# Attention reordered in a hybrid encoder: rotations ahead of scores, values in halves, a second sum buffer, tail masks on TensorE, rstd by product, and a changed cost rule in the static scheduler

## The chip, the cores and the metric

The kernel runs on the eight cores of one Trainium2 chip, one sequence per core, without exchange between the cores. The metric is the device time of the slowest core in microseconds (us). Executions in the usual, fast state agree within about 0.3%. Some executions fall in a slower state, in which the cores of one die get a lower clock; they are marked and left out of every comparison. A ratio is the mean time of one kernel's fast runs over that of the other's of the same rounds, so it isn't quite the ratio of the medians that are quoted.

## The reference, cut to what matters

```python
# x: (8, 2048, 1024); 15 heads of 64 in 3 groups, dilation 1, 4, 16, a band of +-64 keys each
def dilated_attention_mixer(h, w_qkv, q_norm, k_norm, w_o):
    q, k, v = split(h @ w_qkv)
    q = rope(rms_norm(q, q_norm), pos); k = rope(rms_norm(k, k_norm), pos)
    # per group: banded softmax attention over each residue class of positions
    ...
    wts = softmax(stack(lses), axis=0)      # groups weighted by their denominators
    return concat(outs * wts) @ w_o

for i in range(2):                          # layer 0: attention, layer 1: short convolution
    x = x + mixer_i(rms_norm(x))
    x = x + sq_relu_mlp(rms_norm(x))        # 1024 -> 4096 -> 1024
return rms_norm(x)
```

The weights of the groups are proportional to their denominators, so that a group need not be normalized by itself: its exp-weighted values are divided by the sum of all three denominators. The kernel keeps one running sum of denominators (`dtot`) and multiplies by its reciprocal at the end.

## The kernel before: the parts that matter

The program is a list of operations with data ranges, costs and priorities. A list scheduler in Python orders them for each engine before anything runs. The order of each engine's instructions is fixed from then on.

```python
    def schedule(self):
        ...
        while len(order) < n:
            # the engine that can start earliest; on it, the ready operation of lowest priority number
            ...
            o.eng, o.fn, o.cost = alt
            free[e] = t + o.cost
            ...
    def c_dve(n, fast):
        return 0.16 + (0.00053 if fast else 0.00104) * n
```

The heads are worked through in eight units. Units 0 to 5 hold two heads (two lanes) of one group; unit 6 holds two single heads, one with dilation 4 and one with 16; unit 7 holds the last head. A unit's queries and keys are projected, then rotated and normalized (rstd below is the reciprocal root of the mean square, by which they are multiplied):

```python
        def rope_a(u):
            ...                              # swap copy of neighbouring rows by DMA, squares
            MMS(mms, [CRS, sq.r(...)], [PR(b)])          # sums of squares, 8 products of 128x512
            ACT(ln, PS(b), AF.Ln, ...)
            ACT(rs.ap, ln, AF.Exp, ..., scale=-0.5, ps=False)
            DMA("sp", scr_d[u % 2]..., rs.ap[0:61:4, :], ...)          # to DRAM
            for h in range(2):
                DMA("sp", rbc.ap[64 * h:64 * h + 64, 0:n],
                    scr_d[u % 2, h:h + 1, 0:n].broadcast_to([64, n]), ...)   # and back, broadcast
```

The attention of a unit goes in steps of 1024 score columns: scores on PE, exp on ACT, the band mask as a multiplication on DVE, then the output and denominator products on PE into one pair of PSUM banks, which is evicted after each block of 512 positions:

```python
        pp = _Ring([0, 1]); pS = _Ring([2, 4]); pO = (6, 7)       # PSUM banks
        dtot = B(U_DT, 4096, True)
            ...
                ACT(P.ap, psum[:, 512 * sb:512 * sb + 1024], AF.Exp, ..., scale=0.125)
                for (lo, n_, map_, shp) in ml:
                    TT("dve", pv, pv, map_, ALU.mult, ...)         # band mask
        def finalize(units, lo, n):                                # 1/den and its products
            ACT(a, a, AF.Ln, ...); ACT(a, a, AF.Exp, ..., scale=-1.0, ps=False)
            for u in units:
                TT("dve", o, o, dtot.ap[rows, lo:lo + n], ALU.mult, ...)
```

The fillers and the priorities (a lower number goes first):

```python
        p.pri = 1000 * u + 300       # projections and rotation of unit u
        p.pri = 1000 * u             # scores, exp, masks, outputs of unit u
        fill = v_tiles(1, 300); mark = {0: 3}; fill += proj_tiles(1); ...
```

## Time and profile before

| | before |
|---|---|
| time | 1521.54 us median of 3 (1520.95 to 1522.93) |
| PE busy | 95% of the span |
| PE without work, 245 to 330 us | 20 us (median of the cores) |
| TensorE clock at half, 240 to 330 us | 54.6 us (median of the cores) |
| first Relu eviction of the first MLP | 383.2 us (median of the cores) |
| from there to the start of the last matmul | 1124.9 us |

The last two rows cut the run in two, at the first activation of the first MLP. They are read from each core's trace.

The page of the profile, the slowest core (core 6), in 40 equal slices; the digits are tenths busy, and PEclk is the granted TensorE clock in tenths:

```profile
PE 1450.2 (95%) x7207; PEld 675.1 (44%) x7207; DVE 636.2 (42%) x818; ACT 492.5 (32%) x779; POOL 526.7 (35%) x492
...
PE   4999997699999999999998999998999999999996
...
PEclk9999998589999999999999999999999999999998
```

There is one visible hole, around 250 us, with a clock dip. The table of stretches there (columns: stretch in us, its length, then busy time and instruction count of PE, weight load, DVE, ACT, POOL, then the granted clock, the DMA share, GB/s):

```profile
240.00:250.00 10.00, 10.00 (x79) 4.58 (x78) 5.93 (x8) 6.58 (x10) 0.00 (x0) 1.00 0.19 57
250.00:260.00 10.00, 3.70 (x40) 1.82 (x38) 8.16 (x11) 7.44 (x13) 1.61 (x2) 0.71 0.60 118
260.00:270.00 10.00, 4.21 (x12) 1.47 (x12) 6.04 (x11) 1.22 (x3) 0.00 (x0) 0.67 1.10 184
270.00:280.00 10.00, 7.07 (x26) 2.93 (x27) 7.48 (x8) 4.15 (x5) 1.54 (x2) 0.50 0.68 211
280.00:290.00 10.00, 8.37 (x31) 3.55 (x28) 4.96 (x6) 4.05 (x4) 0.75 (x1) 0.50 0.50 173
290.00:300.00 10.00, 6.22 (x23) 2.50 (x22) 5.69 (x6) 3.16 (x3) 2.66 (x5) 0.50 0.61 184
300.00:310.00 10.00, 7.71 (x34) 3.89 (x34) 2.97 (x6) 3.68 (x5) 0.93 (x2) 0.50 0.64 184
310.00:320.00 10.00, 10.00 (x41) 4.17 (x40) 3.47 (x7) 3.50 (x5) 0.75 (x1) 0.72 0.33 107
```

PE is idle in part and at half clock from 270 to 310 us. The chain of work that ended last tells why (start, us, what; in order of time):

```profile
253.48 16.50 DMA arena<-scr
...
271.21 1.23 DVE arena L333
...
272.58 1.10 PE psum L317 x4
...
286.40 1.30 ACT arena L343
...
287.94 2.77 PE psum L317 x8
```

The broadcast read of unit 6's rstd from DRAM takes 16.5 us, then the rotation ends, then PE gets its scores; from there evictions (L343) and 8 output products alternate.

The rest of the run has smaller gaps. The timeline of PE alone after 420 us (start, length, what, count; in brackets the idle time before and what ended it):

```profile
419.71 396.08 PE L317 MATMUL psum<-arena 128*128 128x512 bf16 x1834
818.76 14.19 PE L317 MATMUL psum<-arena 128*128 128x512 bf16 x65 [2.97 <-POOL arena L333]
836.43 208.03 PE L317 MATMUL psum<-arena 128*128 128x512 bf16 x962 [3.48 <-POOL arena L970]
1046.50 14.40 PE L317 MATMUL psum<-arena 128*128 128x512 bf16 x66 [2.04 <-POOL arena L333]
1062.96 429.97 PE L317 MATMUL psum<-arena 128*128 128x512 bf16 x2003 [2.06 <-POOL arena L333]
1496.71 13.22 PE L317 MATMUL psum<-arena 128*128 128x512 bf16 x104 [3.78 <-POOL arena L333]
```

Five gaps, 14.3 us together, each behind a norm. On the median core PE is idle for 11.7 us after 420 us, and its clock is at half for 13.7 us between the first Relu and the last matmul, in periods that begin in these gaps or within 1 us behind them. The timeline of all engines just before the first of them:

```profile
814.62 0.74 DVE L336 SCALAR_TENSOR_TENSOR arena<-arena 128x512 bf16<-128x512 f32 x1
...
815.28 0.68 DVE L333 TENSOR_TENSOR arena<-arena,psum 128x512 f32<-128x512 f32 x1
815.68 2.94 POOL L333 TENSOR_TENSOR arena<-arena 128x512 f32<-128x512 f32 x2 [2.13 <-ACT arena L433]
815.88 3.29 DVE L336 SCALAR_TENSOR_TENSOR arena<-arena 128x512 bf16<-128x512 f32 x2
```

An STT takes 0.74 us while POOL is idle and 1.65 us (3.29 for two) while POOL adds. The scheduler before reckons it as 0.16 + 0.00104 x 512 + 0.06 = 0.75 us in either case. The Trainium skill, "SBUF — State Buffer", section "Who interferes with whom", says that an instruction of the vector engine with two inputs in SBUF contends with a POOL instruction that reads SBUF, since the two share a port. This trace agrees: 0.74 against 1.65 us.

### The profile page before, as it was taken

What the parts mean: (1) busy time and instruction counts of PE and PEld (TensorE: products, weight loads), DVE (VectorE), ACT (ScalarE), POOL (GpSimd) and SP (SyncE); (2) the same over time, 40 slices, a digit from 0 to 9 for tenths busy, and PEclk for the clock granted to TensorE, in tenths of its full rate; (3) what the DMA queues carried; (4) which work ended last, traced back from release to release, by engine and by line L of the source; (5) the groups of instructions that cost most, each with busy time, mean ns of one, the idle gap of its engine ahead of it and who ended that gap; (6) DMA issues with size and microseconds to landing.
All of it is one profiled execution on the core that took longest, in us unless ns stands there. A gap on an engine that the chain in (4) does not pass through costs nothing.

```text
span 1520.2 us, 20021 instructions; the slowest of 8 cores (1513.7 to 1520.2 us)
## 1 busy us (share of the span) xinstructions
PE 1450.2 (95%) x7207; PEld 675.1 (44%) x7207; DVE 636.2 (42%) x818; ACT 492.5 (32%) x779; POOL 526.7 (35%) x492
## 2 busy tenths in 40 slices
PE   4999997699999999999998999998999999999996
PEld 1656443233444444444443444443444444444444
DVE  3647677459413023023049534459223022032058
ACT  3566676343310310310333333333310300301333
POOL 5100000136730630621666222256621621612652
PEclk9999998589999999999999999999999999999998
DMA  9944444630510510411310333311411312213014
GB/s 250 186 91 98 93 110 105 187 85 1 83 29 1 83 28 8 77 29 20 57 22 8 55 42 49 56 29 17 67 28 20 65 28 39 44 28 56 1 56 167
DMA packets 60912, 95.01 MB, mean 62 GB/s; under 512 B 3792, under 2 KB 40912, under 8 KB 58768
## 3 DMA queue, kind: packets, MB, share of 16 engines
q0 software_dynamic: 52016, 69.18, 26.0%
q1 hardware_dynamic: 8800, 24.55, 5.4%
q8 instruction: 60, 0.98, 0.3%
q14 instruction: 36, 0.29, 0.1%
HBM read 127.37 MB, written 8.52 MB: 89 GB/s over the span
## 4 chain that ended last, share of the span: by engine, by line
PE 88%; DVE 4%; DMA 3%; issue 2%; POOL 1%; ACT 1%; SPq 0%; POOLq 0%; DVEq 0%; ACTq 0%
PE psum L317 88%; DVE arena L336 2%; DMA arena<-scr 2%; DMA arena<-xT 2%; DVE arena L333 1%; POOL arena L333 1%; ACT arena L328 1%; POOL arena L349 0%; ACT arena L343 0%; ACT arena L433 0%; SPq L349 0%; DMA outT<-arena 0%; DMA scr<-arena 0%; POOLq L282 0%; POOL arena L449 0%
## 5 line engine op out<-in xcount | busy, mean ns | idle before, releaser
L317 PE MATMUL psum<-arena 128*128 128x512 bf16 (+6 forms) x7207 | 1450.2, 366 | 60.4 <-DVE arena L333 15.3
L317 PEld LDWEIGHTS psum<-arena 128*128 128x128 bf16 (+2 forms) x7207 | 675.1, 101 | 835.3 <-issue 145.5
L333 DVE TENSOR_TENSOR arena<-arena,psum 128x512 f32<-128x512 f32 (+1 forms) x384 | 259.4, 682 | 752.8 <-PE psum L317 749.0
L333 POOL TENSOR_TENSOR arena<-arena 128x512 bf16<-128x512 bf16 (+2 forms) x393 | 449.3, 1147 | 326.8 <-ACT arena L328 144.2
L328 ACT ACTIVATE arena<-psum 128x512 bf16<-128x512 f32 (+1 forms) x306 | 202.0, 668 | 636.6 <-PE psum L317 620.4
L336 DVE SCALAR_TENSOR_TENSOR arena<-arena 128x512 bf16<-128x512 f32 (+2 forms) x232 | 221.2, 995 | 23.1 <-ACT arena L328 18.4
L333 DVE TENSOR_TENSOR arena<-arena 128x2048 bf16<-128x2048 bf16 (+4 forms) x146 | 128.0, 921 | 35.9 <-ACT arena L328 25.1
L349 POOL DMA_DIRECT2D arena<-wdn x16 | 12.5, 781 | 318.6 <-PE psum L317 318.6
L343 ACT CAST arena<-psum 128x512 bf16<-128x512 f32 (+2 forms) x149 | 87.0, 590 | 96.1 <-PE psum L317 91.2
L433 ACT ACTIVATE arena<-arena 128x512 f32<-128x512 f32 x115 | 72.1, 629 | 141.7 <-DVE arena L333 138.3
L328 ACT ACTIVATE arena<-arena 128x512 f32<-128x512 f32 (+2 forms) x85 | 54.3, 656 | 67.8 <-DVE arena L333 55.6
L349 POOL DMA_DIRECT2D arena<-xT x18 | 13.4, 766 | 91.7 <-DVE arena L333 72.4
L349 POOL DMA_DIRECT2D arena<-wqk x8 | 7.4, 925 | 86.8 <-PE psum L317 86.8
L345 DVE CAST arena<-psum 128x512 bf16<-128x512 f32 (+2 forms) x27 | 18.4, 683 | 39.5 <-PE psum L317 39.3
L343 ACT COPY arena<-psum 128x512 f32<-128x512 f32 x38 | 22.8, 600 | 36.7 <-PE psum L317 36.7
L349 POOL DMA_DIRECT2D arena<-wup x16 | 15.0, 938 | 47.2 <-PE psum L317 42.4
L328 ACT ACTIVATE arena<-psum,arena 128x512 f32<-128x512 f32 (+1 forms) x29 | 19.4, 668 | 18.2 <-PE psum L317 18.0
L538 ACT ACTIVATE arena<-arena 128x1024 bf16<-128x1024 bf16 x23 | 24.1, 1057 | 1.9 <-DVE arena L345 0.7
L349 POOL DMA_DIRECT2D arena<-wo x8 | 4.3, 549 | 52.1 <-PE psum L317 52.1
L449 POOL TENSOR_TENSOR arena<-arena 128x512 bf16<-128x512 f32 x8 | 10.8, 1355 | 19.4 <-DMA arena<-xT 19.4
L448 ACT ACTIVATE arena<-arena 128x512 bf16<-128x512 f32 (+1 forms) x30 | 14.2, 525 | 9.9 <-DVE arena L333 6.6
L449 DVE TENSOR_TENSOR arena<-arena 128x512 bf16<-128x512 f32 (+1 forms) x10 | 6.6, 679 | 14.9 <-DMA arena<-xT 14.7
(16 smaller groups left out, 38.6 us busy)
## 6 DMA issues: line engine op xcount, KB each, us to landing
arena<-wup POOLq DMA_DIRECT2D x16, 1024.0 KB, 8.7
arena<-wdn POOLq DMA_DIRECT2D x16, 1024.0 KB, 11.8
arena<-xT POOLq DMA_DIRECT2D x14, 1024.0 KB, 9.2
arena<-arena SPq DMA_DIRECT2D x14, 512.0 KB, 6.3
arena<-scr SPq DMA_DIRECT2D x14, 512.0 KB, 6.6
arena<-win POOLq DMA_DIRECT2D x8, 768.0 KB, 7.4
outT<-arena SPq DMA_DIRECT2D x24, 256.0 KB, 3.0
arena<-wqk POOLq DMA_DIRECT2D x7, 512.0 KB, 11.2
```

What stands on the lines that cost most here:

```text
L317: i = e.matmul(o, lhsT=l, rhs=r, start=s0, stop=s1, skip_group_check=True)
L328: return p.op("act", lambda e: e.activation(out=out, in_=in_, func=func, **kw), R, W, c_act(n, ps) + (0.09 if scale is not None and not is ...
L333: return p.op(eng, lambda e: e.tensor_tensor(out=out, in0=in0, in1=in1, op=op), R, W, cost)
L336: return p.op("dve", lambda e: e.scalar_tensor_tensor(out=out, in0=in0, scalar=scalar, in1=in1, op0=op0, op1=op1), R, W, c_dve(n, False) + ...
L343: alts.append(("act", lambda e: e.copy(out=out, in_=in_), c_act(n) + more))
L345: alts.append((e_, lambda e: e.tensor_copy(out=out, in_=in_), c_dve(n, False) + more))
L349: return p.op(eng, lambda e: e.dma_start(out=out, in_=in_), R, W, 1.3 if eng == "sp" else 1.0, chan=chan, fill=fill, nbytes=nbytes)
L433: p.op([("act", lambda e, o=o, i=xa: e.activation(out=o, in_=i, func=AF.Square), c_act(n, False)), ("dve", lambda e, o=o, i=xa: e.tensor_t ...
L448: alts = [("act", lambda e, o=o, i=xa: e.activation(out=o, in_=i, func=AF.Square), c_act(n, False)), ("dve", lambda e, o=o, i=xa: e.tensor ...
L449: ("dve", lambda e, o=o, i=xa: e.tensor_tensor(out=o, in0=i, in1=i, op=ALU.mult), c_dve(n, False))]
L538: ("act", lambda e, o=sq.ap[:, sl], i_=rw.ap[:, sl]: e.activation(out=o, in_=i_, func=AF.Square), c_act(1024, False))], None, [rw.r(*rr)], ...
```

## The change

The attention's idle time is to be filled, and the scheduler is to know costs that it didn't know. In full the change

- orders units as (group, pair) = (0,0), (1,0), (2,0), (1,1), (0,1), (2,1), takes the values of groups 1 and 2 in halves between the projections, and gives projections, rotations and final products priorities of their own;
- computes the rstd of units 6 and 7 by a block-diagonal product that leaves the mean on all rows, so that Ln and Exp yield the broadcast form without DRAM;
- masks units 4 to 7 by a product of the identity with a bias of 0 or -30000, accumulated before the scores;
- gives unit 7 its own swap and rstd buffers and drops its key copy; gives units 6 and 7 a second sum buffer, on the normed input; moves buffers of x;
- in the scheduler, charges DVE and POOL more when both work from SBUF (contention rule), and doubles PE's cost while its recent load is low (clock rule).

The diff, cut to its core:

```diff
+UNITS = [(0, 0), (1, 0), (2, 0), (1, 1), (0, 1), (2, 1)]
+PMU = 4
+FILL = 'v11 v10 p1 v20 p2 v21 p3 p4 p5 p6 p7'.split()
+AHEAD = [6, 1, 6, 1, 0, 1, 3, 5]
+PRI_P = [-50, 950, 1950, 2950, 3950, 4950, 5950, 6950]
+PRI_R = [-150, -100, 900, 2300, 2900, 4950, 4900, 6650]
+PRI_V = [0, 800, -140]
+PRI_F = [6900, 7900]
+PEB = 6
 ... in schedule():
             o.eng, o.fn, o.cost = alt
+            if o.sbuf and e in both and o.chan is None:
+                over = min(o.cost, max(0.0, both["pool" if e == "dve" else "dve"] - t))
+                o.cost += (0.4 if e == "dve" else 0.15) * over
+                both[e] = t + o.cost
+            if e == "pe":
+                ...                          # load of the last 4 us
+                if full and load < 0.5 and t > 25:
+                    full = False
+                elif load > 0.93:
+                    full = True
+                if not full:
+                    o.cost *= 2
 ... in rope_a():
+            if u >= PEB:
+                for j in range(4 * nw):
+                    b = pp.next()
+                    MMS([(PS(b), bd64.ap, sq.ap[:, sl], True, True)], ...)
+                    ACT(PS(b), PS(b), AF.Ln, ..., 512, bias=eps_ap)
+                    ACT(rbc.ap[:, sl], PS(b), AF.Exp, ..., 512, scale=-0.5)
+                return
 ... in attention():
+                for q in range(2 if on_pe else 0):
+                    mms.append((PS(sb + q), ident.ap, map_, True, False))
-                                    kv(kb.ap[hs(h)]), qv(qb.ap[hs(h)]), True, True))
+                                    kv(kb.ap[hs(h)]), qv(qb.ap[hs(h)]), not on_pe, True))
 ... buffers:
-        dtot = B(U_DT, 4096, True)
+        dtots = [B(U_DT, 4096, True), B(U_HT + 12288, 4096, True)]
+        sws = [B(U_X + 8192, 4096)] * 7 + [B(U_W + 4096, 2048)]
+        rbcs = [B(U_X + 12288, 4096)] * 7 + [B(U_X + 22528, 2048)]
 ... (cuts: loads of the new constants, buffers of x, weight loads held until unit 7 is rotated)
```

More of the change, by code (lines that the diff above doesn't have):

```diff
@@ L25 @@
 CELL = 64
+UNITS = [(0, 0), (1, 0), (2, 0), (1, 1), (0, 1), (2, 1)]
[7 more added lines that the diff above has]
+PEB = 6
 PS_BASE = 1 << 20
 class _Op:
-    __slots__ = ("alts", "eng", "fn", "cost", "chan", "fill", "nbytes", "deps", "idx", "pri",
+    __slots__ = ("sbuf", "alts", "eng", "fn", "cost", "chan", "fill", "nbytes", "deps", "idx", "pri",
                  "pos", "sig", "sig_idx", "succ", "nwait", "ready", "start", "done", "waits")
@@ L61, in op @@
         pe = o.eng == "pe"
+        o.sbuf = all(r[1] < PS_BASE for r in reads)
         rc = list(self.cells(reads))
@@ L109, in schedule @@
         free = {e: 0.0 for e in self.ENGS}
+        both = {"dve": 0.0, "pool": 0.0}
+        hist, h0, full = [], 0, True
         qfree = {"sp": 0.0, "pool": 0.0}
@@ L132, in schedule @@
             o.eng, o.fn, o.cost = alt
+            if o.sbuf and e in both and o.chan is None:
[3 more added lines that the diff above has]
+            if e == "pe":
+                while h0 < len(hist) and hist[h0][1] < t - 4:
+                    h0 += 1
+                load = sum(min(b, t) - max(a, t - 4) for a, b in hist[h0:]) / 4
+                if full and load < 0.5 and t > 25:
[4 more added lines that the diff above has]
+                    o.cost *= 2
+                hist.append((t, t + o.cost))
             free[e] = t + o.cost
@@ L266, in build_nc @@
     cst_d = din("cst", [128, NCST])
+    bd_d = din("bd", [128, 128])
+    bias_d = din("bias", [128, NCST - C_MB + 128])
     rope_d = din("rope", [2, 128, T])
@@ L366, in build_nc @@
         tabs = [B(U_X + 2048 * i, 2048) for i in range(4)]
-        sw = B(U_X + 8192, 4096)
-        rbc = B(U_X + 12288, 4096)
+        sws = [B(U_X + 8192, 4096)] * 7 + [B(U_W + 4096, 2048)]
+        rbcs = [B(U_X + 12288, 4096)] * 7 + [B(U_X + 22528, 2048)]
         sq = B(U_OT + 12288, 4096)
@@ L371, in build_nc @@
         qk = [[B(U_X + 24576 + 2048 * (2 * i + w), 2048) for w in range(2)] for i in range(2)]
+        bd64, ident = B(U_RS + 1024, 128), B(U_RS + 1152, 128)
         rst = [B(U_RS + 512 * i, 512) for i in range(2)]
-        xparts = [[(U_X + 16384, 4), (U_X + 22528, 2), (U_X + 10240, 2)],
-                  [(U_X + 20480, 2), (U_X + 8192, 2), (U_X + 12288, 4)],
+        xparts = [[(U_X + 16384, 4), (U_X + 8192, 4)],
+                  [(U_X + 12288, 4), (U_X + 20480, 4)],
                   [(U_X, 8)], [(U_X + 24576, 8)]]
@@ L404, in xs, with load_w @@
             return b.ap[:, lo:lo + n], b.r(lo, lo + n)
-        def load_w(buf, dview, kc, cols_, chan):
+        def load_w(buf, dview, kc, cols_, chan, after=None):
             o = buf.ap[:, 0:kc * cols_].rearrange("p (c f) -> p c f", c=kc)
-            DMA("pool", o, dview.rearrange("(c p) f -> p c f", p=128), [], [buf.r(0, kc * cols_)],
-                chan, nfill(chan), 128 * kc * cols_ * 4)
+            d = DMA("pool", o, dview.rearrange("(c p) f -> p c f", p=128), [], [buf.r(0, kc * cols_)],
+                    chan, nfill(chan), 128 * kc * cols_ * 4)
+            if after is not None:
+                d.deps.add(after)
             return o
@@ L503, in build_nc @@
             128 * (NCST - C_SEL) * 4)
+        DMA("pool", bd64.ap, bd_d, [], [bd64.r()], "bd", 0, 1 << 16)
         load_wv(1)
@@ L524, in rope_a @@
         def rope_a(u):
-            rw = raws[u % 2]
+            rw, sw, rbc = raws[u % 2], sws[u], rbcs[u]
             nw = 2 if u < 7 else 1
             n = 2048 * nw
-            f = nfill("sw")
+            f = nfill("sw%d" % (u // 7))
             for q in range(2):
                 DMA("sp", sw.ap[q:127 + q:2, 0:n], rw.ap[1 - q:128 - q:2, 0:n], [rw.r(0, n)], [sw.r(0, n)],
-                    "sw", f, 128 * n)
+                    "sw%d" % (u // 7), f, 128 * n)
             for i in range(2 * nw):
@@ L539, in rope_a @@
                        c_act(1024, False))], None, [rw.r(*rr)], [sq.r(*rr)], None)
+            if u >= PEB:
+                for j in range(4 * nw):
+                    b = pp.next()
+                    sl, rr = slice(j * 512, (j + 1) * 512), (j * 512, (j + 1) * 512)
+                    MMS([(PS(b), bd64.ap, sq.ap[:, sl], True, True)], [bd64.r(), sq.r(*rr)], [PR(b)])
+                    ACT(PS(b), PS(b), AF.Ln, [PR(b), sm.r()], [PR(b)], 512, bias=eps_ap)
+                    ACT(rbc.ap[:, sl], PS(b), AF.Exp, [PR(b)], [rbc.r(*rr)], 512, scale=-0.5)
+                return
             b = pp.next()
@@ L558, in rope_a @@
                     [dr], [rbc.r(0, n, h)], "rb", f, 64 * 2 * n)
+        rope_end = {}
         def rope_b(u, which, dst, rows=None):
@@ L563, in rope_b @@
             cs = slice(c0, c1)
-            rw = raws[u % 2]
+            rw, sw, rbc = raws[u % 2], sws[u], rbcs[u]
             for rows_, half, tw in (rows or [(slice(0, 128), 2, which)]):
@@ L571, in rope_b @@
                [rw.r(c0, c1)], 2048, True)
-            TT("dve", dst.ap, rw.ap[:, cs], rbc.ap[:, cs], ALU.mult, [rw.r(c0, c1), rbc.r(c0, c1)], [dst.r()],
-               2048, True)
+            for (d, dh), (rows_, half, _) in zip(dst, rows or [(slice(0, 128), 2, 0)]):
+                d_rows = rows_ if dh == half else slice(64 * dh, 64 * dh + 64)
+                rope_end[u] = TT("dve", d.ap[d_rows], rw.ap[rows_, cs], rbc.ap[rows_, cs], ALU.mult,
+                                 [rw.r(c0, c1, half), rbc.r(c0, c1, half)], [d.r(half=dh)], 2048, True)
         def key_tile(g, kt):
@@ L600, in mask_ap, with attention @@
             return bass.AP(tensor=base.tensor, offset=base.offset, ap=[list(base.ap[0])] + dims)
-        def attention(u, g, lanes, first):
+        def attention(u, g, lanes, first, dtot):
             D = DILS[g]
@@ L686, in evacuate @@
                        [PR(bd), dtot.r(*rng)], [dtot.r(*rng)], 512)
+            m0 = C_MB
+            last = nb - 1
+            on_pe = u >= PMU
             for s in range(16 // per):
@@ L692, in attention @@
                 sb = pS.next()
+                kinds = [0 if (k % (last + 1)) == 0 else (2 if (k % (last + 1)) == last else 1) for k in kts]
+                for q in range(2 if on_pe else 0):
+                    kk = kinds[0:2] if nl == 2 else kinds[2 * q:2 * q + 2]
+                    if D == 16:
+                        map_ = mask_ap(C_M16, [[0, 4], [1, 128]])
+                    elif kk == [1, 1]:
+                        map_ = mask_ap(m0 + 256, [[0, 2], [1, 256]])
+                    else:
+                        map_ = mask_ap(m0 + 256 * kk[0], [[1, 512]])
+                    mms.append((PS(sb + q), ident.ap, map_, True, False))
+                if on_pe:
+                    rd += [CRM, ident.r()]
                 for i, kt in enumerate(kts):
@@ L698, in attention @@
                         mms.append((PS(sb + col // 512, col % 512, col % 512 + ncol),
-                                    kv(kb.ap[hs(h)]), qv(qb.ap[hs(h)]), True, True))
+                                    kv(kb.ap[hs(h)]), qv(qb.ap[hs(h)]), not on_pe, True))
                 for (h, slot, qb, kb) in lanes:
                     rd += [qb.r(half=h), kb.r(half=h)]
-                MMS(mms, rd, [PR(sb, nb=2)], 0.75 if nl == 2 else 1.0)
+                MMS(mms, rd, [PR(sb, nb=2)], 1.0 if nl == 1 or on_pe else 0.75)
                 P = Pb[pP.next()]
                 ACT(P.ap, psum[:, 512 * sb:512 * sb + 1024], AF.Exp, [PR(sb, nb=2)], [P.r()], 1024, scale=0.125)
-                if D == 16:
+                if on_pe:
+                    ml = []
+                elif D == 16:
                     ml = [(0, 1024, mask_ap(C_M16, [[0, 8], [1, 128]]), [8, 128])]
                 else:
-                    m0 = C_MB
-                    last = nb - 1
-                    kinds = [0 if (k % (last + 1)) == 0 else (2 if (k % (last + 1)) == last else 1) for k in kts]
                     if nl == 2:
@@ L742, in attention, with finalize @@
                         out_mms(P_, parts)
-        def finalize(units, lo, n):
+        def finalize(units, lo, n, dtot):
             a, r_ = dtot.ap[:, lo:lo + n], dtot.r(lo, lo + n)
@@ L779, in unit_rope @@
                 for w in range(2):
-                    rope_b(u, w, qk[u % 2][w])
+                    rope_b(u, w, [(qk[u % 2][w], 2)])
             else:
                 a, b_ = qk[u % 2]
-                rope_b(u, 0, a, [(slice(0, 64), 0, 0), (slice(64, 128), 1, 1)])
-                DMA("sp", b_.ap[0:64, :], a.ap[64:128, :], [a.r(half=1)], [b_.r(half=0)], "k7", 0, 1 << 18)
+                rope_b(u, 0, [(a, 0), (b_, 0)], [(slice(0, 64), 0, 0), (slice(64, 128), 1, 1)])
+        def unit_rope(u):
+            rope_a(u)
+            if u < 7:
+                for w in range(2):
+                    rope_b(u, w, [(qk[u % 2][w], 2)])
+            else:
+                a, b_ = qk[u % 2]
+                rope_b(u, 0, [(a, 0), (b_, 0)], [(slice(0, 64), 0, 0), (slice(64, 128), 1, 1)])
         UG = [0, 1, 2, 0, 1, 2]
@@ L791, in one @@
             def one(w, tt):
-                p.pri = 1000 * u + 300
+                p.pri = PRI_P[u]
                 if (w, tt) == (0, 0) and u + 2 < 8:
@@ L805, in unit_att @@
             p.pri = 1000 * u
+            if u == PMU:
+                DMA("pool", cst.ap[:, C_MB:NCST], bias_d[:, 0:NCST - C_MB], [], [CRM], "bias", 0,
+                    128 * (NCST - C_MB) * 4)
+                DMA("pool", ident.ap, bias_d[:, NCST - C_MB:], [], [ident.r()], "ident", 0, 1 << 16)
             q_, k_ = qk[u % 2]
             if u < 6:
-                attention(u, UG[u], [(0, USL[u][0], q_, k_), (1, USL[u][1], q_, k_)], u % 3 == 0)
+                g, pr = UNITS[u]
+                attention(u, g, [(0, 2 * pr, q_, k_), (1, 2 * pr + 1, q_, k_)], u % 3 == 0, dtots[0])
                 if u % 3 == 2:
+                    p.pri = PRI_F[u // 3]
                     for tt in range(4):
-                        finalize([u - 2, u - 1, u], tt * 512, 512)
+                        finalize([u - 2, u - 1, u], tt * 512, 512, dtots[0])
             elif u == 6:
-                attention(6, 1, [(0, 4, q_, k_)], True)
-                attention(6, 2, [(1, 4, q_, k_)], False)
+                attention(6, 1, [(0, 4, q_, k_)], True, dtots[1])
+                attention(6, 2, [(1, 4, q_, k_)], False, dtots[1])
             else:
-                attention(7, 0, [(0, 4, q_, k_)], False)
+                attention(7, 0, [(0, 4, q_, k_)], False, dtots[1])
         wo_t = [B(U_W + 8704 + 1024 * i, 1024) for i in range(7)] + [B(U_V + 10240, 1024)]
@@ L848, in wo_mm @@
                 [oT[u].r(tt * 512, tt * 512 + 512, 0 if u == 7 else 2) for u in us], [PR(b)])
-        fill = v_tiles(1, 300)
-        mark = {0: 3}
-        fill += proj_tiles(1)
-        mark[1] = len(fill) + 3
-        fill += proj_tiles(2)
-        mark[2] = len(fill) + 3
-        fill += v_tiles(2, 2310)
-        for u in range(3, 8):
-            fill += proj_tiles(u)
-            mark[u] = len(fill) + 3
-        fill += [lambda: None] * 4
+        fill, mark = [], {0: AHEAD[0]}
+        for what in FILL:
+            k = int(what[1])
+            if what[0] == "v":
+                h = 8 * int(what[2])
+                fill += v_tiles(k, PRI_V[k])[h:h + 8]
+            else:
+                fill += proj_tiles(k)
+                mark[k] = len(fill) + AHEAD[k]
+        fill += [lambda: None] * 8
         where = {i: u for u, i in mark.items()}
+        assert list(where.values()) == list(range(8)) and sorted(where) == list(where), where
         for i in range(len(fill)):
@@ L866, in build_nc @@
                 u = where[i]
-                p.pri = 1000 * u + 300 if u else -150
+                p.pri = PRI_R[u]
                 unit_rope(u)
@@ L891, in build_nc @@
             p.pri = 8000 + 10 * tt
-            finalize([6, 7], tt * 512, 512)
+            finalize([6, 7], tt * 512, 512, dtots[1])
+        for tt in range(4):
+            p.pri = 8000 + 10 * tt
             for oc in range(8):
@@ L907, in next_slot @@
             wk["n"] += 1
-            return load_w(slots[i], dview, kc, cols_, "w%d" % i), slots[i]
+            after = rope_end[7] if wk["n"] <= 2 else None
+            return load_w(slots[i], dview, kc, cols_, "w%d" % i, after), slots[i]
         aT = [B(U_OT + 8192 * i, 8192) for i in range(2)]
@@ L1067, in _consts @@
     cst[:, C_M16:C_M16 + 128] = np.abs(k[None, :] - k[:, None]) <= 64
-    return cst, rope
+    bd = np.kron(np.eye(2), np.full((64, 64), 1.0 / 64)).astype(np.float32)
+    bias = np.concatenate([-30000.0 * (1.0 - cst[:, C_MB:NCST]), np.eye(128)], axis=1).astype(np.float32)
+    return cst, rope, bd, bias
 def _prep_shared(inp):
@@ L1074, in _prep_shared @@
     wo = f(inp["l0_w_o"])
-    units = [(0, (0, 1)), (1, (0, 1)), (2, (0, 1)), (0, (2, 3)), (1, (2, 3)), (2, (2, 3))]
+    units = [(g, (2 * pr, 2 * pr + 1)) for g, pr in UNITS]
     heads = [[5 * g + s for s in sl] for g, sl in units] + [[9, 14], [4]]
@@ L1104, in _prep_shared @@
             win8[i, :, part * 128:(part + 1) * 128] = win[:, part * 1024 + i * 128:part * 1024 + (i + 1) * 128]
-    cst, rope = _consts()
+    cst, rope, bd, bias = _consts()
     return {
-        "cst": cst, "rope": rope, "sm": sm, "wqk": wqk, "wqk7": f(wqk7), "wv": f(wv), "wo": wo8,
+        "cst": cst, "rope": rope, "bd": bd, "bias": bias, "sm": sm, "wqk": wqk, "wqk7": f(wqk7), "wv": f(wv), "wo": wo8,
         "wup0": f(inp["l0_w_up"]), "wdn0": f(inp["l0_w_down"]),
```

## The prediction

> **What bounds the kernel now.** The page gives PE 95% of a 1520 us span; the chain of waits is 88% PE. In the MLP and convolution stages (390 to 1495 us) the stretch table shows PE full at clock 1.00: 187 matmuls of 128x512 in 40 us, 0.214 us each, with about 15 us of gaps at norm boundaries. The change leaves that arithmetic alone, and the wait for x before 40 us. From 40 to 250 us PE is 99% busy: projections fill the attention's waits.
>
> What can be had is one hole. In the timeline PE stops at 251 us; unit 6 isn't rotated. Its projections ended at 236 us (swap copies issued), but its rstd product ran at 248, behind unit 5's scores, then came a DRAM round trip (the chain charges 16.5 us to the broadcast read, beside loads of x). Scores of unit 6 start at 272.6. PE is idle some 23 us of 250 to 310. The granted clock falls to 0.71, 0.67, then 0.50 from 270 to 310, so the one-lane steps run at half speed: 8 output matmuls of 128x256 take 2.76 us and wait 1.5 us for an eviction. Unit 7 starts at 309; PE is full from there. [...]
>
> I count 63 us (250 to 313) spent on about 21 us of PE work at full clock: the hole is worth 42 us.
>
> **What the change does.**
> - Rotations before scores: unit 6's rstd starts about 9 us earlier. On the path.
> - rstd of units 6 and 7 by a block-diagonal product: 12 matmuls for 12, nothing on PE; no DRAM round trip (up to 20 us); but Ln and Exp on 12 full tiles, about 20 extra activations at 0.6 to 0.65 us, 12 to 13 us of ACT, through two PSUM banks, partly against exponentials.
> - Masks of units 4 to 7 on PE: 22 steps, about 15 us of DVE removed (0.69 each), 44 products of 128x512 added, 44 x 0.214 = 9.4 us of PE. In units 4 and 5 PE is full, so 5 us of it is paid; in 6 and 7 part hides in eviction waits.
> - Unit 7 without the key copy, with own swap and rstd buffers: it rotates under unit 6.
> - Second sum buffer, products last: DVE and ACT are free of them while unit 6 starts, but they must still fit. The new buffer lies on the normed input, so unit 6's first sum waits for the last projection.
> - Values in halves: filler order only.
>
> **Sum.** 42 - 9 of the hole, plus 2 of small gaps at 170 to 192, minus remaining bubbles: one output bank pair (1 to 1.5 us per eviction, 12 of them), rotation of unit 7 (9 us of DVE plus 8 us of swap copy) under some 20 us of unit 6. I take 9 us for them. Unit 7 would start near 282 us rather than 309; gain about 26 us.
>
> Predicted 1495 us, range 1484 to 1511. Faster by over 2% (below 1491) 0.33, within 2% 0.63, slower 0.04.
>
> **Right if:** the clock stays near 1.0 through 250 to 310; no broadcast read in the chain there; unit 6's scores start before 262 us; from the MLP on the trace is the old one shifted. DVE busy falls about 15 us, ACT rises about 12.
> **Wrong if:** bubbles in units 6 and 7 still drop the clock to half (then nearer 1508); ACT saturates with rstd and exponentials; x or weight loads, now later, hold the output projection; or all bubbles close (below 1488).

## More of the kernel before

At each boundary between sublayers the down projection's products of a column chunk are added to x (8 adds on DVE), squared (ACT), summed over the rows (7 adds on POOL and one product with ones on PE), and the normed chunk is written by 8 scalar_tensor_tensor instructions (STT) on DVE, while PE is already in the next chunk:

```python
            TT("dve", xa, xa, PS(b, 0, n), ALU.add, ...)              # add_x
            TT("pool", d, acc.ap[:, 0:n], o, ALU.add, ...)            # square_sum
            STT(h_ap(c, c0, n), src[0], gain, nb_.ap[:, 0:n], ALU.mult, ALU.mult, ...)   # norm_to_hT
```

## The result, and the profile after

The changed kernel takes 1497.07 us (median of 4 runs, 1495.32 to 1524.36, of which one slow), beside 1521.38 us for the kernel before. The ratio of the fast runs is 0.9835, with a 95% interval of 0.9815 to 0.9854: faster by 1.65%, inside 2%.

| median of the cores, us | before | changed | difference |
|---|---|---|---|
| first score product of unit 6 | 270.1 | 256.6 | -13.5 |
| first score product of unit 7 | 304.3 | 278.8 | -25.5 |
| first Relu of the first MLP | 383.2 | 372.6 | -10.6 |
| from there to the start of the last matmul | 1124.9 | 1109.3 | -15.6 |
| PE without work, 245 to 330 us | 20.0 | 5.1 | -14.9 |
| clock at half, 240 to 330 us | 54.6 | 27.3 | -27.3 |

The time fell by as much as predicted, but not where it was predicted to. Only 10.6 us came out of the attention; 15.6 us came out of stages whose arithmetic the change doesn't touch. The same lines of the profile as above (the slowest core is core 0 now), first the page:

```profile
PE 1448.1 (97%) x7115; PEld 676.5 (45%) x7251; DVE 629.1 (42%) x806; ACT 495.9 (33%) x788; POOL 527.1 (35%) x493
...
PE   4999999999999999999999999999999999999996
...
PEclk9999999699999999999999999999999999999998
```

The stretches (same columns):

```profile
250.00:260.00 10.00, 9.24 (x87) 4.32 (x87) 6.73 (x10) 8.65 (x13) 1.50 (x2) 1.00 0.45 161
260.00:270.00 10.00, 9.84 (x53) 3.97 (x53) 6.49 (x7) 5.88 (x8) 0.75 (x1) 0.93 0.93 311
270.00:280.00 10.00, 8.36 (x27) 3.10 (x28) 5.87 (x6) 6.65 (x10) 1.70 (x4) 0.50 0.44 151
280.00:290.00 10.00, 9.78 (x34) 3.70 (x36) 6.22 (x11) 6.24 (x10) 1.69 (x3) 0.50 0.98 225
290.00:300.00 10.00, 10.00 (x49) 4.50 (x48) 4.51 (x9) 2.85 (x5) 1.17 (x2) 0.87 0.79 179
300.00:310.00 10.00, 9.48 (x48) 4.20 (x46) 4.40 (x7) 4.06 (x6) 0.47 (x1) 1.00 0.01 2
310.00:320.00 10.00, 7.27 (x24) 2.64 (x24) 6.14 (x10) 3.10 (x5) 0.42 (x1) 0.66 0.70 105
```

PE is nearly always occupied, and still the clock falls to half from about 269 to 293 us, and once more near 313. The chain of work has no broadcast read any more; evictions and PE alternate:

```profile
254.06 0.70 DVE arena L382
...
256.83 7.61 PE psum L354 x57
...
274.84 1.30 DVE arena L382
...
276.37 12.90 PE psum L354 x42
```

PE alone after 420 us:

```profile
419.75 1050.89 PE L354 MATMUL psum<-arena 128*128 128x512 bf16 x4791
1471.04 13.04 PE L354 MATMUL psum<-arena 128*128 128x256 bf16 x104 [0.40 <-POOL arena L370]
```

The five gaps behind the norms are gone. The timeline of DVE and POOL for the same column chunk as in the one shown of before:

```profile
799.59 0.68 DVE L370 TENSOR_TENSOR arena<-arena,psum 128x512 f32<-128x512 f32 x1
800.19 1.16 DVE L373 SCALAR_TENSOR_TENSOR arena<-arena 128x512 bf16<-128x512 f32 x1
...
801.25 1.27 POOL L370 TENSOR_TENSOR arena<-arena 128x512 f32<-128x512 f32 x1 [0.45 <-ACT arena L475]
801.27 0.67 DVE L370 TENSOR_TENSOR arena<-arena,psum 128x512 f32<-128x512 f32 x1
801.87 1.20 DVE L373 SCALAR_TENSOR_TENSOR arena<-arena 128x512 bf16<-128x512 f32 x1
```

Adds to x (L370) and STTs (L373) alternate one by one, where before two STTs in a row stood ahead of the next add. Counted from the first Relu of its core, the last add of this chunk starts at 428.5 us, against 430.4 before.

The scheduler's list shows the same. Below is DVE's order at the end of the first MLP for one column chunk and the norm of the chunk ahead of it (A = add to x of the later chunk, S = STT of the earlier). This is a listing of the schedule and not a profile:

```
before:   A1 A1 A1 A1 S0 S0 A1 S0 A1 S0 S0 A1 S0 A1 S0 S0
changed:  A1 A1 A1 A1 S0 S0 A1 S0 A1 S0 A1 S0 A1 S0 S0 S0
```

The last add of chunk 1 (counted from 0) stands behind six STTs before and behind five after. Its square, POOL's sum and the product with ones on PE hang on that add. The next chunk, whose product with ones waits at 818.76 us before, has the same counts; there the changed list also puts one of the running sums of squares on DVE. PE's list differs too, but not at every gap: for the last chunk of the first MLP and of the convolution, the product with ones stands one group of eight products (8 x 0.214 = 1.7 us) later than before. At the other three gaps its place is unchanged, so there the order on the other engines alone closed the gap.

### The profile page after: what moved, and what is told of

Same layout as the page of the kernel before. It is cut to its first block, busy times and chain, and to the rows that moved or that the text cites. A ratio compares the mean times of both kernels' runs of the same rounds, so it can differ in the third digit from the quotient of the medians.

```text
span 1494.8 us, 19962 instructions; the slowest of 8 cores (1490.7 to 1494.8 us)
## 1 busy us (share of the span) xinstructions
PE 1448.1 (97%) x7115; PEld 676.5 (45%) x7251; DVE 629.1 (42%) x806; ACT 495.9 (33%) x788; POOL 527.1 (35%) x493
## 4 chain that ended last, share of the span: by engine, by line
PE 92%; DVE 3%; issue 2%; DMA 2%; POOL 0%; ACT 0%; DVEq 0%; ACTq 0%; POOLq 0%
PE psum L354 92%; DVE arena L373 2%; DMA arena<-xT 2%; DVE arena L370 1%; POOL arena L386 0%; DVE arena L382 0%; ACT arena L380 0%; POOL arena L491 0%; ACT arena L490 0%; ACT arena L840 0%; DVE arena L491 0%; ACT arena L365 0%; DVE arena L476 0%; DVEq L251 0%; DVEq L319 0%
## 5 line engine op out<-in xcount | busy, mean ns | idle before, releaser
L354 PE MATMUL psum<-arena 128*128 128x512 bf16 (+6 forms) x7115 | 1448.1, 365 | 36.0 <-ACT arena L490 14.9
L370 DVE TENSOR_TENSOR arena<-arena,psum 128x512 f32<-128x512 f32 (+1 forms) x384 | 258.2, 679 | 741.1 <-PE psum L354 726.0
L370 POOL TENSOR_TENSOR arena<-arena 128x512 bf16<-128x512 bf16 (+2 forms) x393 | 449.3, 1147 | 316.3 <-ACT arena L365 139.9
L365 ACT ACTIVATE arena<-psum 128x512 bf16<-128x512 f32 (+1 forms) x318 | 209.2, 668 | 620.0 <-PE psum L354 583.6
L373 DVE SCALAR_TENSOR_TENSOR arena<-arena 128x512 bf16<-128x512 f32 (+2 forms) x232 | 222.7, 1004 | 12.4 <-ACT arena L365 7.4
L370 DVE TENSOR_TENSOR arena<-arena 128x2048 bf16<-128x2048 bf16 (+4 forms) x123 | 112.0, 959 | 27.9 <-DMA arena<-arena 12.9
L380 ACT CAST arena<-psum 128x512 bf16<-128x512 f32 (+2 forms) x143 | 82.1, 578 | 89.7 <-PE psum L354 86.4
L382 DVE CAST arena<-psum 128x512 bf16<-128x512 f32 (+2 forms) x33 | 24.4, 739 | 48.7 <-PE psum L354 48.7
L386 POOL DMA_DIRECT2D arena<-wup x16 | 15.0, 939 | 37.4 <-PE psum L354 27.3
## 6 DMA issues: line engine op xcount, KB each, us to landing
arena<-wup POOLq DMA_DIRECT2D x16, 1024.0 KB, 10.5
arena<-wqk POOLq DMA_DIRECT2D x7, 512.0 KB, 11.7
```

Source lines behind the costliest of these rows:

```text
L354: i = e.matmul(o, lhsT=l, rhs=r, start=s0, stop=s1, skip_group_check=True)
L365: return p.op("act", lambda e: e.activation(out=out, in_=in_, func=func, **kw), R, W, c_act(n, ps) + (0.09 if scale is not None and not is ...
L370: return p.op(eng, lambda e: e.tensor_tensor(out=out, in0=in0, in1=in1, op=op), R, W, cost)
L373: return p.op("dve", lambda e: e.scalar_tensor_tensor(out=out, in0=in0, scalar=scalar, in1=in1, op0=op0, op1=op1), R, W, c_dve(n, False) + ...
L380: alts.append(("act", lambda e: e.copy(out=out, in_=in_), c_act(n) + more))
L382: alts.append((e_, lambda e: e.tensor_copy(out=out, in_=in_), c_dve(n, False) + more))
```

## The experiments

All kernels gave correct results. The ratio is against the kernel before, run on the same chip beside them. "First Relu" and "rest" are the two parts of the table above, each a median over the cores of the profiled run.

### e1: the contention rule alone

```diff
 kernel before, schedule():
+            if o.sbuf and e in both and o.chan is None:
+                over = min(o.cost, max(0.0, both["pool" if e == "dve" else "dve"] - t))
+                o.cost += (0.4 if e == "dve" else 0.15) * over
+                both[e] = t + o.cost
```

> The kernel before, with only the rule in its static scheduler that charges DVE and POOL more when both work from SBUF; no attention edit, no clock rule. Theory A (the gain after the attention, about 15 us between the first MLP's last relu and the end, comes from this rule, which places the norm work later in PE's order): about 1507 us, ratio 0.990 to 0.992, PE gaps behind the norms gone (14 us before), first relu of MLP 0 still near 383 us. Rival B (the later gain comes from the attention edits or from the x layout): within 3 us of before. Rival C (it comes from the clock rule): within 3 us of before.

Measured: 1506.52 us median, ratio 0.9895 (0.9876 to 0.9915). First Relu at 381.8 us (1.4 earlier), rest 1109.4 us (15.5 less). The timeline of PE alone after 420 us, of this kernel:

```profile
419.77 1061.46 PE L325 MATMUL psum<-arena 128*128 128x512 bf16 x4937
1481.42 13.26 PE L325 MATMUL psum<-arena 128*128 128x512 bf16 x105 [0.18 <-POOL arena L341]
```

Theory A holds: four lines of a cost model, with not one instruction more or less in the arithmetic, make the whole later gain and nearly two thirds of the total. Rivals B and C fall. On the median core the idle time after 420 us falls from 11.7 to 0.6 us, and the 13.7 us at half clock are gone. The rule needn't be exact: it prices an STT that lies wholly beside POOL at 0.75 x 1.4 = 1.05 us, and the trace had 1.65. What closed the gaps is the new order that came of it. At the two gaps where PE's order moved too, no run takes the two shares apart.

### e2: the clock rule alone

```diff
 kernel before, schedule():
+            if e == "pe":
+                ...
+                if not full:
+                    o.cost *= 2
```

> The kernel before, with only the rule that doubles PE's cost in the scheduler when its recent load was low. Theory A: the later stages stay as before (1060.8 - 769 us from last relu of MLP 0 to first of MLP 1, about 291 us); the total within 4 us of before, the attention a little better or worse. Rival C (this rule makes the later gain): that stretch falls to about 281 us and the total by 10 to 15 us.

Measured: 1530.14 us, ratio 1.0052 (1.0034 to 1.0069), so slower. First Relu at 387.8 us (4.6 later), rest 1126.1 us (1.2 more). The rule has no part in the later gain, and on the old attention it does harm.

### e3: the changed kernel without both rules

```diff
 changed kernel, schedule():
-            if o.sbuf and e in both and o.chan is None: ...
-            if e == "pe": ...
```

> The changed kernel with both scheduler rules taken out, all attention edits kept. Theory A: the stretch from MLP 0's last relu to MLP 1's first goes back from 281 to about 291 us, and the end from 70 to about 75 us: about 1511 us, ratio to before near 0.993, which would then be all that the attention edits are worth. Rival B: stays near 1497 us.

Measured: fast runs of 1518.71, 1523.13 and 1523.51 us (a fourth was slow), ratio 0.9998 (0.9975 to 1.0020). First Relu at 377.1 us (6.1 earlier than before), rest 1127.8 us (2.9 more than before). The expectation of 0.993 was too high: the attention edits save 6.1 us up to the first Relu, and the gaps behind the norms take part of it back (PE is idle for 14.9 us after 420 us on the median core, 11.7 before). Without the scheduler's rules the edits are worth nothing that these rounds can tell from zero.

### e4: masks on DVE again

```diff
-PMU = 4
+PMU = 8
```

> The changed kernel with the masks of all units on VectorE again (no mask products on TensorE). If masks on PE help by freeing VectorE and by keeping PE's activity up: 2 to 8 us slower than the changed kernel (1499 to 1505 us). If the 44 added products of 0.214 us are simply paid on a full PE (my prediction took 5 of 9.4 us as paid): 3 to 6 us faster (about 1492 us). The first relu of MLP 0 is the mark: 372.6 us in the changed kernel.

Measured: 1497.26 us, ratio 0.9840 (0.9820 to 0.9859), the same as the changed kernel's 0.9835. First Relu 374.1, rest 1109.5 us. Neither expectation was met: it isn't slower by 2 us or more, and not faster. The marks show why. The last score product of unit 5 came at 247.5 us, against 254.0 with masks on PE, so the products were paid in units 4 and 5 (24 products, 24 x 0.214 = 5.1 us). But unit 6's first scores came at 257.1 us, against 256.6, so the time that PE saved was spent waiting. The added products stood in a wait. The clock was at half for 51.2 us between 240 and 330 us, against 27.3 in the changed kernel, at nearly the same first Relu.

### e5: rstd of units 6 and 7 through DRAM again

```diff
-PEB = 6
+PEB = 8
```

> The changed kernel with the rstd of units 6 and 7 through DRAM again. My prediction: the round trip was on the path, so unit 6 starts later and the first relu of MLP 0 moves from 372.6 us to 380 or later, total 1503 to 1510 us. Rival: with the rotation now ahead of the scores, the round trip hides behind unit 5 and the twenty fewer activations pay for it: within 3 us of the changed kernel (1497).

Measured: 1496.52 us, ratio 0.9833 (0.9814 to 0.9853). First Relu 372.4, rest 1109.2 us, unit 6's first scores at 255.7 us against 256.6. The rival holds as to the time. For unit 6 the round trip hides: on core 0 its broadcast reads are issued at 238.3 and 238.9 us, and the later lands at 246.5, after 7.6 us. In the kernel before it took 16.5, where the median of its 14 reads of this size was 6.6; so 16.5 was not the cost of the method but of that moment. Whether the late start or the transfers beside it made it long isn't tested. For unit 7 the round trip doesn't hide: its reads land at 266.7 us, DVE waits for them, and PE waits behind DVE for 4.6 to 6.0 us once on each core. PE's waits for DVE from 250 to 320 us (total, times, longest), first of this kernel, then of the changed one:

```profile
PE psum L354 <- DVE arena L370: 6.9, 2, 6.0
...
PE psum L354 <- DVE arena L370: 2.6, 4, 1.5
```

By the first Relu that wait has been made up; where, the runs don't show.

### e6: the old priorities

```diff
-PRI_P = [-50, 950, 1950, 2950, 3950, 4950, 5950, 6950]
-PRI_R = [-150, -100, 900, 2300, 2900, 4950, 4900, 6650]
+PRI_P = [1000 * u + 300 for u in range(8)]
+PRI_R = [-150] + [1000 * u + 300 for u in range(1, 8)]
```

> The changed kernel with the old priorities of projections and rotations (all at 1000u+300; unit order, filler order and the rest as changed). If rotations before scores carry most of what the attention gained (372.6 against 381.8 us of the first relu with the scheduler rule alone): back to about 381 us, total about 1506 us. Rival (the block-diagonal rstd and the free DVE carry it): within 3 us of 1497.

Measured: fast runs of 1501.12 and 1502.26 us (two others were slow), ratio 0.9866 (0.9842 to 0.9890). First Relu at 378.9 us, 6.3 later than in the changed kernel, rest 1109.2 us; unit 6's first scores at 261.3 us, 4.7 later. The priorities carry most of the attention's gain, though not all of the expected 8.

### e7: one sum buffer

```diff
-        dtots = [B(U_DT, 4096, True), B(U_HT + 12288, 4096, True)]
+        dtots = [B(U_DT, 4096, True), B(U_DT, 4096, True)]
```

> The changed kernel with one sum buffer, so that the first eviction of unit 6 waits for Ln, Exp and the products of units 3 to 5, which come last by priority. Expected: a new wait of some 5 to 15 us in front of unit 6's second block, the clock at half from there, 1504 to 1512 us. If the products hide anyway: within 3 us of 1497.

Measured: 1501.12 us median, ratio 0.9859 (0.9840 to 0.9879). First Relu 377.8 us, 5.2 later, rest 1108.9 us. The expectation was right in direction, but the total lies below the expected 1504 to 1512. PE's longest wait for DVE from 250 to 320 us is 3.7 us, against 1.5 in the changed kernel, and the clock is at half for 30.7 us, against 27.3. With the products last, the second buffer is worth these 5.2 us.

### e8: mask products of units 6 and 7 repeated

```diff
+                    for _ in range(1 if u < 6 else 3 if D < 16 else 5):
                         mms.append((PS(sb + q), ident.ap, map_, True, False))
```

> The changed kernel with each mask product of units 6 and 7 issued three times (five times for dilation 16) into the same bank, each overwriting the last: same result, 48 more products of 128x512, 10 us at full clock. Theory (in units 6 and 7 the half clock, 267 to 293 us, is the loss, and it comes from a PE that is too little occupied between the evictions): the clock stays at 1.0 for most of that stretch and the added work is paid back: total within 4 us of 1497 or below. Rival (PE waits for evictions, or the clock falls for another reason): the added work is paid, at half clock 10 to 20 us: 1507 to 1517.

Measured: 1500.14 us median, ratio 0.9853 (0.9834 to 0.9873). First Relu 376.3 us (3.7 later), rest 1109.1 us. The clock was at half for 8.5 us instead of 27.3. The stretches of this kernel (same columns as above):

```profile
260.00:270.00 10.00, 10.00 (x58) 3.96 (x56) 7.82 (x8) 5.70 (x9) 1.46 (x2) 1.00 0.90 299
270.00:280.00 10.00, 10.00 (x37) 4.39 (x36) 5.20 (x8) 3.10 (x6) 0.04 (x1) 0.83 0.34 122
280.00:290.00 10.00, 7.96 (x31) 3.06 (x30) 6.00 (x7) 6.98 (x9) 1.37 (x3) 0.83 0.28 105
```

More work on PE does hold the clock, so the cause of the dip is right: too little activity between evictions. Three kernels agree: with no mask products in units 6 and 7 (e4, which has none in units 4 and 5 either) the clock was at half for 51.2 us, with 20 (changed) for 27.3, with 68 (here) for 8.5. And 48 x 0.214 = 10.3 us of useless products cost only 3.7 us of time. But the clock alone doesn't pay: if all of the 18.8 us fewer at half clock had been PE-bound, 9.4 us would have come back and the kernel would have been slower by about 1 us. The first Relu came at 374.1, 372.6 and 376.3 us in these three, so the time at half clock doesn't rank them. The total lies within the 4 us that the theory allowed, but its premise, that the half clock is the loss, isn't borne out.

### e9 and e10: an attempt to beat both

The output projection's part of units 0 to 5 for two of four chunks is done early, as filler for units 6 and 7, and added to x separately. In e10 the mask products of units 6 and 7 are doubled besides (threefold for dilation 16).

```diff
+        for tt in (0, 1):
+            p.pri = 7600
+            for oc in range(8):
+                b = pp.next()
+                wo_mm(b, oc, tt, range(6), None)
+                add_x(tt, oc, 0, 512, b)
```

> A version meant to beat both: the changed kernel, with the output projection's part of units 0 to 5 for the first two of four column chunks done early, in its own sum that is added to x separately (16 more adds on VectorE, 0.68 us each), as filler for PE in units 6 and 7, through the two banks that the projections used. If PE's spare time and half clock there (27 us at half) are the loss: clock back earlier, first relu of MLP 0 5 us earlier than 372.6, total about 1491 us (ratio 0.980). Rival (VectorE, which has the evictions, rotation and products there, is the limit): within 2 us of 1497 or slower.

> The same with each mask product of units 6 and 7 issued twice (three times for dilation 16), 20 more products. If the clock rather than PE's work is the limit there, this is faster than the early projection alone, by up to 4 us; if the early projection already holds the clock, it is slower by up to 4 us.

(By its edit e10 adds 24 products, not 20: 16 once more and 4 twice more.)

Measured: e9 1505.77 us, ratio 0.9895 (0.9878 to 0.9912); e10 1509.76 us, ratio 0.9921 (0.9902 to 0.9941). Both are slower than the changed kernel. In e9 PE's idle time from 245 to 330 us fell to 2.3 us, but the first Relu came at 374.0 us all the same, and the rest grew to 1117.9 us. The timeline of PE alone in e9 shows the new waits:

```profile
360.59 5.33 PE L354 MATMUL psum<-arena 128*128 128x512 bf16 x22 [1.06 <-DVE arena L370]
...
370.58 18.37 PE L354 MATMUL psum<-arena 128*128 128x512 bf16 x72 [3.55 <-DVE arena L370]
394.05 26.25 PE L354 MATMUL psum<-arena 128*128 128x512 bf16 x110 [5.09 <-DVE arena L373]
```

DVE was busy for 10.00 of every 10 us from 350 to 390 us in this kernel. The rival holds: a filler on PE that costs DVE 16 adds moves the wait to DVE. The last wait is for 8 STTs that take 19.25 us (2.4 us each), while POOL makes 12 adds in 13.14 us beside them. e10, the slower of the two, was at half clock for 10.2 us from 240 to 330 us, e9 for 20.5, so the clock isn't the limit there either.

### e11: the changed kernel without the clock rule

```diff
 changed kernel, schedule():
-            if e == "pe": ...
```

> The changed kernel without the scheduler's clock rule, the contention rule kept. With both rules gone the changed kernel lost 4.5 us up to the first relu of MLP 0 (377.1 against 372.6) and 18 us after it. If the contention rule makes all of the later gain: the stretches after the first relu stay as in the changed kernel (381.6 us to 281.3 us and so on, within 2 us in sum), and the total is within 5 us of 1497, by what the clock rule does in the attention. Rival (the clock rule has a part in the later gain once the attention is changed): PE gaps behind the norms come back, total 1505 us or more.

Measured: 1510.79 us, ratio 0.9913 (0.9895 to 0.9931). On this chip die 1 ran up to 0.8% longer than die 0 (median spans 1504.9 and 1498.6 us in the profiled run). The trace shows why: cores 4 to 7 were granted a clock of 0.81 for 30.0 to 60.1 us, in periods of 15.0 us, and cores 0 to 3 never. So I read die 0. There the first Relu came at 381.3 us (371.8 on die 0 of the changed kernel), and the rest took 1107.3 us (1109.3). The later gain stays with the contention rule alone, as expected. But the clock rule is worth 9.5 us up to the first Relu in the changed attention (7.3 by the median of all eight cores; 5.8 in the median span of die 0 over all fast runs), more than the 5 expected, although on the attention before it cost 4.6 us (e2). With neither rule the first Relu came at 377.1 us (e3), so the contention rule alone makes the changed attention later. What a rule does to one list says little about another list.

### e12: masks on DVE and rstd through DRAM together

```diff
-PMU = 4
-PEB = 6
+PMU = 8
+PEB = 8
```

> The changed kernel with both the masks on VectorE and the rstd of units 6 and 7 through DRAM, so without the two rewritings of arithmetic. Each alone made no difference (0.9840 and 0.9833 against 0.9835). If they are worth nothing because the rotation of unit 6 and the evictions set the pace whichever engine does this work: within 3 us of 1497. If each only stands in for the other (PE work filling the same time): slower, 1501 to 1510 us.

Measured: the two fast runs took 1505.98 and 1506.59 us (two others were slow), ratio 0.9877 (0.9856 to 0.9898). It is the same chip as in e11, with die 1 longer (1500.3 us against 1492.3) and again at a clock of 0.81 for 45.1 to 60.1 us on cores 4 to 7 alone. On die 0, which was undisturbed, the median span is 1492.3 us against 1491.8 for the changed kernel, the first Relu came at 372.8 us (371.8), and the rest took 1109.5 us (1109.3). On that die the two rewritings of arithmetic together are worth nothing measurable, although the clock was at half for 54.6 us from 240 to 330 us there (23.9 on die 0 of the changed kernel); the time of the whole chip doesn't settle it, because of die 1.

## Why the prediction was right, and where it was wrong

The time was right: 1495 us predicted, 1497.07 measured, and the class (within 2%, given 0.63) too. The sum was right through two errors that cancel: 26 us were expected from the attention, of which 10.6 came, and nothing from the later stages, of which 15.6 came. That the two cancelled was luck.

- **"From the MLP on the trace is the old one shifted": wrong.** The prediction listed the gaps behind the norms (15 us) as untouched, since the arithmetic there is untouched. It passed over the scheduler's part of the diff without pricing it. e1, e3 and e11 show that the contention rule closes these gaps: 15.5 us on the kernel before. The evidence stood in the profile of before: 0.74 us for an STT alone and 1.65 us beside POOL, against 0.75 us in the scheduler in either case.
- **"The clock stays near 1.0 through 250 to 310": wrong.** It was at half for 27.3 us. "I take 9 us for them" (the remaining bubbles) is the term that was mis-sized. Measured were 5.1 us of idle PE and 27.3 us at half clock, worth up to 13.7 us, so up to 18.8 us in place of 9. That is an upper bound and no more: e4 reached nearly the same first Relu with 9.2 us idle and 51.2 at half clock, and e12 on die 0 with 10.5 and 54.6. What the bubbles really cost stays open. The list of what could go wrong named this case; the central estimate didn't carry it.
- **"Unit 7 would start near 282 us": right by its mark, and misleading.** Its first scores came at 278.8 us. But in the kernel before the first scores of unit 7 came when unit 6 was finished and PE was full from there on; in the changed one unit 7's scores are interleaved with unit 6's outputs, and PE has half clock and gaps until about 319 us. Of the 25.5 us at this mark 10.6 were left at the first Relu. A start is a poor mark when the change interleaves.
- **Unit 6's scores before 262 us, no broadcast read in the chain: right** (256.6 us; the chain shows none).
- **"No DRAM round trip (up to 20 us)": wrong as a saving.** Through DRAM the first Relu comes at 372.4 us instead of 372.6 (e5). For unit 6 the early start of the rotation had already hidden it; for unit 7 it cost a wait of 4.6 to 6.0 us that was made up elsewhere.
- **Masks: "5 us of it is paid": right where it was put, without effect.** Unit 5's last scores came 6.5 us later for it, and unit 6's rotation absorbed it (e4). DVE fell by 7.1 us (636.2 to 629.1) rather than 15, and ACT rose by 3.4 rather than 12, in part because the scheduler moved copies between them (DVE's copies out of PSUM take 30.4 us, before 23.8).
- **Priorities and second sum buffer: right in kind.** Taking back either costs 6.3 (e6) and 5.2 us (e7) up to the first Relu. They depend on each other, and so do the rules, so these numbers don't add up to 10.6.

The prediction had the clock back at about 313 us. The trace has it back at 315.6, and with that the hole is worth some 43 us rather than 42.

Open: with 42 us for the hole, 2 for small gaps, 9.4 for the masks and up to 18.8 for what remained, 16 us would have been left for the attention, and 10.6 were measured. The other 5 us have no experiment. A likely place is that PE "busy" in units 6 and 7 contains waits for evictions, since the ends of matmuls are modelled; that would also fit e8, where a clock held high returned less than its share. This is argued and not shown. The order of the units, the values in halves, unit 7's own buffers and the moved buffers of x were not taken back one by one either.

No version beat the changed kernel. e4 and e5 equal it with less new code, and so does e12 on the undisturbed die.

## What to carry to other kernels

When an order is made by a cost model, compare the model's cost of each operation with the trace's, alone and beside the engines that run with it. A wrong price shows up far from the place of the change, and putting it right can be worth more than rewriting the arithmetic. Price every part of a diff, the part that "only schedules" too. Before adding work to remove a latency, try whether an earlier start hides it, and before filling an idle engine, ask which other engine the filler loads.

## What the Trainium skill lacked or had wrong

- "TensorE: Matmul & The Clock Gate", "HAM oscillation — how this bites in real kernels", gives as the abstract rule that PE must have no idle gaps above about 3.4 us. As a rule to go by it isn't enough; the page's next section, "A second HAM failure mode: psum-queue depth-cycling", does say that frequent short idle times between groups of matmuls make the clock oscillate, but not how short or how frequent. On core 0 of the changed kernel the clock fell to half at 268.7 us with no gap over 0.6 us in the 25 us before it, and it fell like that on six of the eight cores (matmul ends are modelled in the trace, so short waits can hide in them). Little work between evictions was enough, and added products held the clock (e8).
- The same page, Part 1, is borne out on the two states of its table and its window of 3413 ns: the median core was at half clock for 27.3 us (8 windows) and before the change for 54.6 us (16 windows), and the single periods were 6.83, 17.07 and 23.89 us in the changed kernel. A clock of 0.81 stands in the traces of e9 to e12 alone, for 4.9 to 60.1 us of a run on the cores that have it.
- "SBUF — State Buffer", "Who interferes with whom", says which instructions contend and that the loser blocks; it gives two ratios of slowing (6.8 and 1.5 times) without a duration, and none for these two operations side by side. Here an STT went from 0.74 to 1.65 us, or to 1.16 to 1.20 us when it alternated with adds from PSUM, and a POOL add from 1.27 to about 1.47 us.
- No page says that a static order made with uncontended costs can cost 1% of a kernel: 15.9 us of 1522 here (e1).
